# A decoder layer on one core: the way back's first four tiles normed together and turned chunk by chunk, the second gate's columns moved into the mixing

## The chip, the core and the metric

The kernel runs on one core of a Trainium2 chip. The core has a matrix engine (TensorE, PE in the profile; PEld is its weight load), VectorE (DVE), ScalarE (ACT), GpSimd (POOL) and SyncE (SP), whose queue issues most of the kernel's DMAs. The metric is the device time of one execution in microseconds, lower is better; several executions are timed and the median stands for the kernel.

## The reference

One hybrid decoder layer over 1024 tokens of width 1024, in float32. c is one conditioning vector; nine vectors of shifts, scales and gates come from it.

```python
mod = c_act @ w_ada + b_ada
(sh1, sc1, ga1, sh2, sc2, ga2, sh3, sc3, ga3) = jnp.split(mod, N_MOD, axis=-1)

h = modulate(rms_norm(x, g_pre_ff1), sh1, sc1)
f = swiglu(h, w1_gate, w1_up, w1_down)                 # 1024 -> 2816 -> 1024
x = x + 0.5 * ga1[:, None, :] * rms_norm(f, g_post_ff1)

h = modulate(rms_norm(x, g_pre_mix), sh2, sc2)
proj = h @ w_in                                        # q, k, v and u
attn = sliding_window_attention(q, k, v, sinks)        # window 128, 8 query heads, 2 kv heads
ssm = s5_ssm(u, ...)                                   # diagonal complex state space, GELU, GLU
mixed = jnp.concatenate([rms_norm(attn, g_attn_out), rms_norm(ssm, g_ssm_out)], -1) @ w_out
x = x + ga2[:, None, :] * rms_norm(mixed, g_post_mix)

h = modulate(rms_norm(x, g_pre_ff2), sh3, sc3)
x = x + 0.5 * ga3[:, None, :] * rms_norm(swiglu(h, w2_gate, w2_up, w2_down), g_post_ff2)
```

## The kernel before

The tokens are eight tiles of 128 (t = 0 to 7); the width is eight chunks of 128 (k = 0 to 7). Memory on the chip is divided by hand into named slots: `a0` to `a27`, `q`, `r`, `w` and `c0` hold 4 KB per partition, `h` and `t` 2 KB, and eight PSUM banks `b0` to `b7` hold 512 columns of float32 each. A tile asked for under a name waits until the last user of that slot is done. A planner works through the program with costs of its own and lays out one order of instructions for each engine ahead of time; on the chip every engine, and SP's queue of DMAs, keeps that order. `pinned` (line 85) ties instructions to the order in which they are written.

Each float32 product is made of three matmuls of rounded parts (`mm3`, lines 74 to 76). `split` (lines 69 and 70) makes the parts: ACT casts to the high part, DVE subtracts it from the source for the low part. So every operand that PE takes has first one pass of ACT and one of DVE.

The order of the work is: first half-step up (gate and up products), first way back (`down` with n = 0), mixing (`mix`), second half-step up, second way back (`down` with n = 2). Both half-steps use a scheme of seven products for a 2 by 2 block matrix product. The way back runs six of them ("1", "2", "6", "5", "3", "7"), each in 11 steps s of 12 matmuls, and the seventh in twelve pieces, three for each of tiles 4 to 7 (lines 621 to 639). The upper halves (`hi`, columns 512 to 1023) of tiles 0 to 3 are finished after "3" (line 612), so all of these four tiles stand in `f[0]` to `f[3]` before "7" begins. The upper halves of tiles 4 to 7 are finished after "7" (line 617), their lower halves piece by piece.

`epilogue` (lines 246 to 259) norms one whole tile: sum of squares on ACT, root and reciprocal in tiny steps (`rsqrt`, lines 141 to 145), product with the gate row `grow` on DVE, addition to x (line 255), store, and for n = 0 a second norm and a scaling (line 259) for the mixing. The four of them are listed in `todo` and run at odd steps of "7". `epilogue_half` (lines 261 to 288) does this for tiles 4 to 7, the upper half ahead of time with its gain product on POOL (line 269), the lower in `finish` after DVE copied PSUM into the tile (line 632).

For the mixing every tile is turned by PE (`to_mix`: four transposes into one bank, line 205), scaled and shifted into a staging tile, 128 columns at a time (ACT line 241, DVE line 243), and split into the operands `hm` (`split_mix`); tiles 0 to 3 share one staging tile and are split chunk by chunk when all four are in. `to_mix_` lists these steps, and the loop over the pieces takes one after each piece. The mixing then projects the first half of the tokens, which is tiles 0 to 3, with six weights (`project(i, 0)`), then the second half. The weights come through `ins`, a stream of loads (line 659) and splits; `before_mix` makes its first three loads and its first split, and is called after the tenth piece, with two small steps for the second gate before them.

`hook2` runs in each step of the way back. From the sixth step of "6" on it loads the second gate's weight columns (w_ada 40 to 47) as sixteen halves into `h` slots and reduces each with c on DVE (`ada_half`, line 171). The mixing's first loads into `a24` and `a25` are the attention's bias (line 736). Its scores begin after three projections of the second half.

Of the kernel before, what the change touches and what calls it, by code (L numbers as in the profile page):

```python
# [30 lines left out]
def tile_layer(ctx: ExitStack, tc: tile.TileContext, a: dict, out: bass.AP, stage: str = "all"):  # L31
# [212 lines left out]

    def split_mix(ts, stage, hm, ks):
        for k in ks:
            split(*(by_j(x[k], 16 * ts[0], 16 * len(ts)) for x in hm), by_j(stage[k], 0, 16 * len(ts)))
# [13 lines left out]
    def epilogue_half(n, t, f, grow, x_tag, j_tag, g_tag, normed):  # L261

        xt, junk, g = slot(x_tag, [D]), slot(j_tag, [D]), slot(g_tag, [D])
        sp.dma_start(xt, x_d[n][t])
        halves = slice(0, 512), slice(512, D)
        ss = small(2, "ssh")
        lo, hi = halves
        act.activation(junk[:, hi], f[:, hi], AF.Square, accum_out=ss[:, 1:2])
        pool.tensor_tensor(g[:, hi], f[:, hi], grow[:, hi], op=MUL)
        dve.tensor_scalar(ss[:, 1:2], ss[:, 1:2], 1.0 / D, EPS, op0=MUL, op1=ADD)  # L270

        def finish():
            act.activation(junk[:, lo], f[:, lo], AF.Square, accum_out=ss[:, 0:1])
            dve.tensor_tensor(g[:, lo], f[:, lo], grow[:, lo], op=MUL)
            v = small(1, "ssv")
            dve.scalar_tensor_tensor(v, ss[:, 0:1], 1.0 / D, ss[:, 1:2], op0=MUL, op1=ADD)
            r = rsqrt(v, 1)
            if normed:
                dve.scalar_tensor_tensor(xt, g, r[:, 0:1], xt, op0=MUL, op1=ADD)
                sp.dma_start(x_d[n + 1][t], xt)  # L280
                r = row_rstd(xt, f)
                act.activation(f, xt, AF.Identity, scale=r[:, 0:1])
            else:
                for h, eng in zip(halves, (sp, act)):
                    dve.scalar_tensor_tensor(xt[:, h], g[:, h], r[:, 0:1], xt[:, h], op0=MUL, op1=ADD)
                    eng.dma_start(x_d[n + 1][t][:, h], xt[:, h])

        return finish
# [211 lines left out]
    def down(n, wd, then, hook, last):  # L500
# [4 lines left out]
        raw_rots = [Rot(*names("a", 20, 21, 22, 23)), Rot(*names("a", 11, 12, 13, 14, 15, 27)), o_rot]  # L505
# [69 lines left out]
        todo = []  # L575
        for s in range(ns):
# [12 lines left out]
            if m == "7":  # L589
                late_ops[i] = slot(f"a{16 + i}", [2, 512], F32R)  # L590
                split(late_ops[i][:, 0], late_ops[i][:, 1], L[i][:, 1])
                if i % 2 and todo:
                    todo.pop(0)()
                if i == NH_F - 3:
                    upto("lload", 2, len(pieces), last_load)
                if i >= NH_F - 2:
                    upto("lconv", i - NH_F + 3, len(pieces), last_conv)
            if i < NH_F - 1:
                continue
            for t in range(4):  # L600
# [10 lines left out]
                elif m == "3":  # L611
                    dve.tensor_tensor(f[t][:, hi], f[t][:, hi], pbs[t], op=ADD)
                    if t == 0:
                        grow = load_row(n, "c0")
                    todo.append(lambda t=t: epilogue(n, t, f[t], grow, f"a{11 + t}", "a15", f"a{t}", then is not None))
                elif m == "7":
                    dve.tensor_tensor(f[4 + t][:, hi], f[4 + t][:, hi], pbs[t], op=ADD)
        for g in todo:
# [65 lines left out]
    def mix_streams():  # L684
# [8 lines left out]
        return Stream(ins, Rot(*names("r", 2, 3, 0, 1)), 3), Stream(us, Rot("w2", "w3"), 1), Stream(late, Rot("a14", "a15", "a14", "a15", "r0", "c0", "r0", "c0"), 1), Stream(shares, Rot(*names("w", 0, 1, 2, 3)), 3)  # L693

    def mix(hm, st, st_u, late, shares, todo, start):
# [25 lines left out]

        for j, i in enumerate(QKV):
# [721 lines left out]
    late_ada, late_raw = [(j, h) for j in range(40, 48) for h in range(2)], []  # L1444

    def hook2(s):

        i = s % NH_F
        if s < NH_F:
            if i == NH_F // 2:  # L1450
                for _ in prep[0]:
                    pass
# [11 lines left out]
    late_c = []  # L1464
# [7 lines left out]
    def to_mix_(f, t):  # L1472
# [4 lines left out]
        ts = [t for t in {0: (0, 1, 2, 3), 4: (4, 5), 5: (4, 5)}.get(t, (t,))]  # L1477
# [11 lines left out]
        todo = [lambda t=t, b=b: steps(t, b) for t in (ts if t == 0 else [t]) for b in range(2)]  # L1489
# [4 lines left out]
    def before_mix():  # L1494
        gate_row(1, 5, False)
        gate_store(1)
# [118 lines left out]
```

## Time and profile before

| | |
|---|---|
| median of 3 runs | 1712.78 us (1706.69 to 1713.24) |
| the profiled execution | 1704.67 us, span 1702.9 us |
| PE busy | 1649.9 us, 97% of the span |
| DVE, ACT, POOL busy | 1264.4 us (74%), 803.6 us (47%), 120.7 us (7%) |
| HBM | 145 GB/s over the span |

The span is the time from the first to the last instruction of the profiled execution. Busy times are sums over the whole layer, whose stages have different limits. In the rows below times are counted from the span's start.

### The profile page before, as it was taken

Reading aid. Unit: us, or ns where it says so; the run is one execution under the profiler, and the core shown is the slowest. Engines: PE = TensorE matmul, PEld = TensorE weight load, DVE = VectorE, ACT = ScalarE, POOL = GpSimd, SP = SyncE. Lnnn points to the kernel's source line nnn. Section 1 sums busy time; section 2 is a strip of 40 time slices with the busy share of each in tenths; the row PEclk is TensorE's granted clock in tenths of the full one; section 3 lists DMA queues with packets and bytes.
Section 4 is the critical chain, followed back from the end, with each engine's and each line's share of the span. In section 5 each row is a group of like instructions: output and inputs, shape, how many; then the busy total and the mean of one; then the engine's idle time right before and its main releaser. Section 6 shows DMA issues by size and latency. Waiting matters only on the chain.

```text
span 1702.9 us, 22218 instructions
## 1 busy us (share of the span) xinstructions
PE 1649.9 (97%) x7669; PEld 1353.3 (79%) x7669; DVE 1264.4 (74%) x2470; ACT 803.6 (47%) x1654; POOL 120.7 (7%) x147
## 2 busy tenths in 40 slices
PE   6999999999999999899989998999999999999998
PEld 5888888787788878788767886878888888888886
DVE  7999988789779878735589368777666566678586
ACT  5633333553344557736564257633333333444462
POOL 0011100001100000000014053000000000000001
PEclk8999999999999999999999998999999999999999
DMA  9186742234495733410233126253322223493324
GB/s 382 40 284 232 257 163 94 105 135 148 137 355 189 231 121 136 163 36 15 90 97 87 50 81 200 75 201 106 117 94 93 93 101 123 158 377 114 112 97 163
DMA packets 112066, 249.08 MB, mean 146 GB/s; under 512 B 12089, under 2 KB 27745, under 8 KB 111953
## 3 DMA queue, kind: packets, MB, share of 16 engines
q1 hardware_dynamic: 102224, 214.12, 36.6%
q0 software_dynamic: 9152, 32.49, 5.7%
q8 instruction: 60, 0.98, 0.2%
q10 hardware_dynamic: 576, 1.05, 0.2%
q14 instruction: 54, 0.43, 0.1%
HBM read 187.87 MB, written 59.75 MB: 145 GB/s over the span
## 4 chain that ended last, share of the span: by engine, by line
PE 50%; DVE 5%; ACT 2%; DMA 1%; issue 1%; SPq 0%; POOL 0%; DVEq 0%; ACTq 0%; POOLq 0%
PE b L76 15%; PE b L75 15%; PE b L74 15%; PE b L751 1%; PE b L839 1%; PE b L841 1%; DVE a L70 1%; PE b L840 1%; PE b L930 1%; PE b L785 1%; PE b L926 1%; ACT a L69 0%; PE b L205 0%; DMA r<-in_w_gu 0%; DMA w<-in_w_out 0%
## 5 line engine op out<-in xcount | busy, mean ns | idle before, releaser
L75 PE MATMUL b<-a,w 128*128 128x512 f32 x1260 | 493.5, 392 | 5.0 <-DVE a L70 5.0
L74 PE MATMUL b<-a,w 128*128 128x512 f32 x1260 | 489.2, 393 | 8.6 <-ACT w L69 3.5
L76 PE MATMUL b<-a,w 128*128 128x512 f32 x1260 | 494.2, 392 | 3.2 <-DVE w L70 3.1
L74 PEld LDWEIGHTS b<-a,w 128*128 128x128 f32 x1260 | 238.0, 189 | 61.6 <-ACT w L69 3.9
L76 PEld LDWEIGHTS b<-a,w 128*128 128x128 f32 x1260 | 238.3, 189 | 55.6 <-DVE w L70 5.9
L75 PEld LDWEIGHTS b<-a,w 128*128 128x128 f32 x1260 | 238.2, 189 | 55.1 <-DVE a L70 6.1
L70 DVE TENSOR_TENSOR w<-r,w 128x512 fp32r<-128x512 f32 (+1 forms) x206 | 142.9, 694 | 128.6 <-ACT w L69 128.3
L75 PE MATMUL b<-w,r 128*128 128x512 f32 x528 | 205.5, 389 | 1.7 <-DVE w L70 1.7
L76 PE MATMUL b<-w,r 128*128 128x512 f32 x528 | 205.4, 389 | 0.0
L74 PE MATMUL b<-w,r 128*128 128x512 f32 x528 | 180.7, 389 | 0.0
L69 ACT CAST w<-r 128x512 fp32r<-128x512 f32 (+1 forms) x210 | 130.2, 623 | 91.8 <-DVE r L334 82.1
L69 ACT CAST r<-a 128x512 fp32r<-128x512 f32 x110 | 68.5, 623 | 148.9 <-PE b L76 112.0
L70 DVE TENSOR_TENSOR r<-a,r 128x512 fp32r<-128x512 f32 x110 | 75.7, 688 | 60.3 <-ACT r L69 59.9
L75 PEld LDWEIGHTS b<-w,r 128*128 128x128 f32 x528 | 99.1, 188 | 22.7 <-DVE w L70 2.1
L76 PEld LDWEIGHTS b<-w,r 128*128 128x128 f32 x528 | 99.1, 188 | 20.6
L74 PEld LDWEIGHTS b<-w,r 128*128 128x128 f32 x528 | 99.1, 188 | 20.5
L69 ACT CAST w<-t 128x512 fp32r<-128x512 f32 (+1 forms) x114 | 69.9, 613 | 87.4 <-DVE t L337 33.5
L70 DVE TENSOR_TENSOR w<-t,w 128x512 fp32r<-128x512 f32 (+1 forms) x114 | 79.7, 699 | 32.4 <-ACT w L69 32.1
L466 DVE TENSOR_TENSOR h<-h,b 128x512 f32<-128x512 f32 x120 | 82.1, 685 | 20.4 <-PE b L76 18.6
L454 ACT ACTIVATE h<-h 128x512 f32<-128x512 f32 x60 | 38.0, 633 | 117.8 <-DVE h L466 117.8
L70 DVE TENSOR_TENSOR w<-a,w 128x512 fp32r<-128x512 f32 x110 | 75.4, 685 | 0.4 <-ACT w L69 0.4
L74 PE MATMUL b<-a,a 128*128 128x512 f32 x182 | 72.0, 398 | 0.0
(376 smaller groups left out, 2548.2 us busy)
## 6 DMA issues: line engine op xcount, KB each, us to landing
r<-in_w_gu SPq DMA_DIRECT2D x88, 512.0 KB, 4.1
g_d<-h SPq DMA_DIRECT2D x154, 256.0 KB, 2.2
a<-g_d SPq DMA_DIRECT2D x110, 256.0 KB, 3.4
q<-in_w_ada POOLq DMA_DIRECT2D x48, 512.0 KB, 4.6
a<-in_w_d SPq DMA_DIRECT2D x88, 256.0 KB, 5.4
a<-in_w_ada SPq DMA_DIRECT2D x16, 512.0 KB, 10.1
a<-in_x SPq DMA_DIRECT2D x12, 512.0 KB, 5.9
x_d<-a SPq DMA_DIRECT2D x12, 512.0 KB, 3.8
```

Source lines behind the costliest of these rows:

```text
L69: act.copy(hi, src)
L70: eng.tensor_tensor(lo, src, hi.bitcast(F32), op=SUB)
L74: pe.matmul(psum, wh, xh, start=first, stop=False, skip_group_check=goes_on)
L75: pe.matmul(psum, wh, xl, start=False, stop=False, skip_group_check=goes_on)
L76: pe.matmul(psum, wl, xh, start=False, stop=last, skip_group_check=goes_on)
L454: act.activation(dst, src, AF.Silu)
L466: dve.tensor_tensor(dst, dst, pb, op=ADD)
L751: pe.matmul(pb[kv][:, m % 2, ks], qT[m][rows, t * P : (t + 1) * P], kT[rows, (t + 1 - nk) * P : (t + 1) * P], start=True, stop=True,)
L785: pe.transpose(pt[:, m, :], pr[4 * kv + m][:, b * P : (b + 1) * P], ident)
L839: pe.matmul(pb, hh, wh, start=k == 0, stop=False)
L840: pe.matmul(pb, hh, wl, start=False, stop=False)
L841: pe.matmul(pb, hl, wh, start=False, stop=k == NK - 1)
```

## The change

Tiles 0 to 3 are no longer normed one by one. `epilogue_four` takes the sums of squares and gain products in halves: the lower halves while "5" runs, the upper in "7", each half in place in `f`; one root and reciprocal serves all four tiles, and a second one their second norm. Its steps are popped two at a step in "7". `to_mix_four` turns one chunk of all four tiles into one bank (`b4` to `b7`), evicts 512 columns by one instruction, on ACT or DVE in turn, and splits them at once; three such steps are popped after each of the first three pieces. `epilogue_half` works in place, makes its gain product on DVE and reads the lower half from PSUM without a copy. `before_mix` is called after the fifth piece.

The second gate's columns leave `hook2`. They are loaded whole, four at a time into `a24` to `a27`, in the mixing after the six projections of the first half, and reduced by `gate_columns` behind the remaining steps of the last tile, which are now pinned; the bias follows into `a24` and `a25`. The stream of projection weights has three slots instead of four. The slots of the "7" loads, of the half epilogues and of `grow` (loaded at the first step of "6") change with this. Both ways back use the new code; only the first has the second norm and the turning.

```diff
+    def to_mix_four(k, f, hm, rot):
+        pt = bank(f"b{4 + k % 4}", [4, P])
+        for t in range(4):
+            pe.transpose(pt[:, t, :], f[t][:, k * P : (k + 1) * P], ident)
+        stage = slot(rot(), [512])
+        dst = stage.rearrange("p (j t l) -> p t j l", j=8, t=4)
+        src = pt.rearrange("p t (j l) -> p t j l", j=8)
+        scale, shift = gsc[:, 1, k : k + 1], mod(3)[:, k : k + 1]
+        if k % 2:
+            dve.tensor_scalar(dst, src, scale, shift, op0=MUL, op1=ADD)
+        else:
+            act.activation(dst, src, AF.Identity, scale=scale, bias=shift)
+        split(*(by_j(x[k], 0, 64) for x in hm), by_j(stage, 0, 64))
...
+    def epilogue_four(n, f, grow, junks, x_tags, junk_tag, normed):
+        halves = slice(0, 512), slice(512, D)
+        ss = small(8, "ss4")
+        X = {}
+        def part(h, t):
+            junk = slot(junks(), [512])
+            act.activation(junk, f[t][:, halves[h]], AF.Square, accum_out=ss[:, 4 * h + t : 4 * h + t + 1])
+            dve.tensor_tensor(f[t][:, halves[h]], f[t][:, halves[h]], grow()[:, halves[h]], op=MUL)
+        def loads():
+            for t in range(4):
+                X[t] = slot(x_tags[t], [D])
+                sp.dma_start(X[t], x_d[n][t])
+        def first_norm():
+            v = small(4, "ssv4")
+            dve.tensor_tensor(v, ss[:, 0:4], ss[:, 4:8], op=ADD)
+            X["r"] = rstd_of(v, 4, D)
+            X["ss"] = small(4, "ssn4")
+        def add(t):
+            dve.scalar_tensor_tensor(X[t], f[t], X["r"][:, t : t + 1], X[t], op0=MUL, op1=ADD)
+            sp.dma_start(x_d[n + 1][t], X[t])
+            if normed:
+                act.activation(slot(junk_tag, [D]), X[t], AF.Square, accum_out=X["ss"][:, t : t + 1])
+        def second_norm():
+            X["r"] = rstd_of(X["ss"], 4, D)
+        def scaled(t):
+            act.activation(f[t], X[t], AF.Identity, scale=X["r"][:, t : t + 1])
...
         act.activation(junk[:, hi], f[:, hi], AF.Square, accum_out=ss[:, 1:2])
-        pool.tensor_tensor(g[:, hi], f[:, hi], grow[:, hi], op=MUL)
+        dve.tensor_tensor(f[:, hi], f[:, hi], grow[:, hi], op=MUL)
...
-        def finish():
-            act.activation(junk[:, lo], f[:, lo], AF.Square, accum_out=ss[:, 0:1])
-            dve.tensor_tensor(g[:, lo], f[:, lo], grow[:, lo], op=MUL)
+        def finish(pb):
+            act.activation(junk[:, lo], pb, AF.Square, accum_out=ss[:, 0:1])
+            dve.tensor_tensor(f[:, lo], pb, grow[:, lo], op=MUL)
...
-        raw_rots = [Rot(*names("a", 20, 21, 22, 23)), Rot(*names("a", 11, 12, 13, 14, 15, 27)), o_rot]
+        raw_rots = [Rot(*names("a", 20, 21, 22, 23)), Rot(*names("a", 11, 12, 13, 14, 15, 27)), Rot(*names("h", *range(6)))]
...
+        on_first, on_both = epilogue_four(
+            n, f, lambda: grow, Rot("h6", "h7"), names("a", 11, 12, 13, 14), "a15", then is not None)
...
-                if i % 2 and todo:
-                    todo.pop(0)()
+                for _ in range(2 if i < 6 else 1):
+                    if on_both:
+                        on_both.pop(0)()
...
+            if s == 2 * NH_F:
+                grow = load_row(n, "c0")
+            if m == "5" and i % 2 and on_first:
+                on_first.pop(0)()
...
-                tags = (f"q{t % 2}", "w3" if t < 2 else "q2", ("r0", "r2", "r3", "q3")[t])
+                tags = (("r0", "q0", "q1", "q0")[t], ("r3", "q2", "q3", "q2")[t])
...
-                dve.tensor_copy(y[:, lo], pb[0][t])
-                finish()
+                finish(pb[0][t])
...
-            if todo:
-                todo.pop(0)()
-            if s == len(pieces) - 3:
+            for _ in range(3 if s < 3 else 1):
+                if todo:
+                    todo.pop(0)()
+            if s == 4:
                 last()
...
-        return Stream(ins, Rot(*names("r", 2, 3, 0, 1)), 3), ...
+        return Stream(ins, Rot(*names("r", 2, 3, 0)), 2), ...
...
+        gate_ada, gate_raw = list(range(40, 48)), []
+        gate_rot = Rot(*names("a", 24, 25, 26, 27))
+        def gate_load(n_):
+            while gate_ada and len(gate_raw) < n_:
+                j = gate_ada.pop(0)
+                w = slot(gate_rot(), [D])
+                sp.dma_start(w, a["w_ada"][j])
+                gate_raw.append((j, w))
...
                 for f in todo[: 4 if j == 0 else None]:
-                    f()
+                    pinned(f)
                 todo = todo[4:]
+        gate_load(4)
         project(0, 1)
+        def gate_columns():
+            gate_c = load_c(sp)
+            for j in range(40, 48):
+                ada_block(*gate_raw.pop(0), gate_c)
+                gate_load(4)
+            gate_row(1, 5, False)
+        pinned(gate_columns, hold=False)
         project(1, 1)
+        gate_store(1)
...
-        elif s >= 2 * NH_F + 4:
-            if not late_c:
-                late_c.append(load_c(sp))
-            while late_ada and len(late_raw) < 4:
-                j, h = late_ada.pop(0)
-                w = slot(f"h{(2 * j + h) % 8}", [512])
-                tc.keep_in_program_order(sp.dma_start(w, a["w_ada"][j][:, 512 * h : 512 * h + 512]))
-                late_raw.append((j, h, w))
-            if s >= 2 * NH_F + 8 and late_raw:
-                ada_half(*late_raw.pop(0), late_c[0])
...
+            rot = Rot("h6", "h7")
+            return [lambda k=k: to_mix_four(k, f, hm, rot) for k in range(NK)]
...
     def before_mix():
-        gate_row(1, 5, False)
-        gate_store(1)
         ins.load(3)
         ins.conv(0)
```

## Rows read from the trace of the kernel before

**Rows 1.** The page, busy time of an engine, share of the span, instructions.

```profile
PE 1649.9 (97%) x7669; PEld 1353.3 (79%) x7669; DVE 1264.4 (74%) x2470; ACT 803.6 (47%) x1654; POOL 120.7 (7%) x147
```

**Rows 2.** Windows by stage: length, busy us (x count) by engine, granted clock, DMA.

```profile
595.50:625.50 30.00, 28.28 (x125) 23.08 (x124) 17.18 (x29) 14.42 (x27) 0.00 (x0) 1.00 0.53 167
625.50:655.50 30.00, 30.00 (x134) 24.83 (x133) 27.14 (x53) 22.31 (x41) 0.00 (x0) 1.00 0.10 40
655.50:690.85 35.35, 35.35 (x173) 29.45 (x172) 29.26 (x88) 27.84 (x68) 5.54 (x4) 1.00 0.56 181
690.85:705.25 14.40, 9.47 (x34) 7.35 (x33) 10.98 (x35) 11.46 (x24) 0.56 (x1) 0.76 0.79 268
...
729.90:754.00 24.10, 24.10 (x111) 19.44 (x111) 0.11 (x1) 3.00 (x6) 0.00 (x0) 1.00 0.13 44
```

**Rows 3.** Timeline of PE: start, length, line, operation, count, idle time before <-releaser.

```profile
690.85 0.27 PE L185 MATMUL b<-ident,ggc 128*8 128x128 f32 x1
690.96 0.60 PE L205 MATMUL b<-ident,q 128*128 128x128 f32 x4
695.03 0.50 PE L74 MATMUL b<-a,w 128*128 128x512 f32 x1 [3.47 <-ACT w L69]
...
697.66 0.80 PE L76 MATMUL b<-a,w 128*128 128x512 f32 x1 [1.46 <-DVE w L70]
...
703.22 0.39 PE L74 MATMUL b<-a,w 128*128 128x512 f32 x1
...
705.25 0.39 PE L74 MATMUL b<-a,q 128*128 128x512 f32 x1
```

**Rows 4.** Timeline of ACT, 689.0 to 698.5.

```profile
689.59 4.25 ACT L69 CAST a<-h 128x512 fp32r<-128x512 f32 x8
...
693.94 1.04 ACT L69 CAST w<-r 128x1024 fp32r<-128x1024 f32 x1
```

**Rows 5.** Timeline of DVE, 689.0 to 698.5.

```profile
696.40 1.21 DVE L70 TENSOR_TENSOR w<-r,w 128x1024 fp32r<-128x1024 f32 x1
```

**Rows 6.** Timeline of PE, 596.0 to 599.5.

```profile
598.89 0.50 PE L75 MATMUL b<-w,r 128*128 128x512 f32 x1 [1.72 <-DVE w L70]
```

**Rows 7.** Timeline of DVE, 593.0 to 600.0.

```profile
596.67 0.75 DVE L171 CUSTOM_DVE_ANT_0 h<-h,c,modc 128x512 f32<-128x512 f32 x1 [0.97 <-DMA h<-in_w_ada]
```

**Rows 8.** Timeline of all engines at the span's end.

```profile
1695.38 0.69 DVE L632 COPY q<-b 128x512 f32<-128x512 f32 x1 [1.76 <-PE b L76]
1696.11 0.63 ACT L273 ACTIVATE q<-q 128x512 f32<-128x512 f32 x1 [4.72 <-DVE q L632]
1696.11 0.69 DVE L274 TENSOR_TENSOR q<-q,c 128x512 f32<-128x512 f32 x1
...
1696.86 0.16 DVE L276 SCALAR_TENSOR_TENSOR s<-s 128x1 f32<-128x1 f32 x1
```

**Rows 9.** DVE's groups, 625.5 to 731: count | busy us, mean ns | idle before.

```profile
L243 DVE TENSOR_SCALAR h<-b,gsc,modc 128x128 f32<-128x128 f32 x28 | 9.7, 402 | 2.8 <-PE b L205 2.8
...
L255 DVE SCALAR_TENSOR_TENSOR a<-a,s,a 128x1024 f32<-128x1024 f32 x4 | 5.1, 1283 | 0.1
...
L254 DVE TENSOR_TENSOR a<-q,c 128x1024 f32<-128x1024 f32 x4 | 4.9, 1218 | 0.0
```

**Rows 10.** ACT's groups, the same stretch.

```profile
L241 ACT ACTIVATE h<-b,modc,gsc 128x128 f32<-128x128 f32 x28 | 10.5, 451 | 1.9 <-PE b L205 1.9
```

**Rows 11.** Line 166, whole gate columns: ns least/median/most, first and last start.

```profile
L166 DVE CUSTOM_DVE_ANT_0 q<-q,c,cols x48: 1276/1280/1286, 97.7 to 1169.3; 128x1024 f32<-128x1024 f32 x48
```

**Rows 12.** DMA issues, 680 to 760: count, KB each, median us to landing.

```profile
a<-in_k_bias SPq DMA_DIRECT2D x2, 512.0 KB, 5.9
```

**Rows 13.** DMA issues, 540 to 600.

```profile
h<-in_w_ada SPq DMA_DIRECT2D x16, 256.0 KB, 3.8
```

**Rows 14.** Timeline of ACT, 631 to 634.

```profile
631.48 1.28 ACT L141 ACT_TABLE_LOAD   x1
```

More of the change, by code (lines that the diff above doesn't have):

```diff
@@ L259, in epilogue, with epilogue_half @@
             act.activation(f, xt, AF.Identity, scale=r[:, 0:1])
-    def epilogue_half(n, t, f, grow, x_tag, j_tag, g_tag, normed):
-        xt, junk, g = slot(x_tag, [D]), slot(j_tag, [D]), slot(g_tag, [D])
+    def epilogue_four(n, f, grow, junks, x_tags, junk_tag, normed):
[24 more added lines that the diff above has]
+            act.activation(f[t], X[t], AF.Identity, scale=X["r"][:, t : t + 1])
+        on_first = [lambda t=t: part(0, t) for t in range(4)]
+        on_both = [loads] + [lambda t=t: part(1, t) for t in range(4)] + [first_norm] + [lambda t=t: add(t) for t in range(4)]
+        if normed:
+            on_both += [second_norm] + [lambda t=t: scaled(t) for t in range(4)]
+        return on_first, on_both
+    def epilogue_half(n, t, f, grow, x_tag, j_tag, normed):
+        xt, junk = slot(x_tag, [D]), slot(j_tag, [D])
         sp.dma_start(xt, x_d[n][t])
@@ L278, in finish @@
             if normed:
-                dve.scalar_tensor_tensor(xt, g, r[:, 0:1], xt, op0=MUL, op1=ADD)
+                dve.scalar_tensor_tensor(xt, f, r[:, 0:1], xt, op0=MUL, op1=ADD)
                 sp.dma_start(x_d[n + 1][t], xt)
@@ L284, in finish @@
                 for h, eng in zip(halves, (sp, act)):
-                    dve.scalar_tensor_tensor(xt[:, h], g[:, h], r[:, 0:1], xt[:, h], op0=MUL, op1=ADD)
+                    dve.scalar_tensor_tensor(xt[:, h], f[:, h], r[:, 0:1], xt[:, h], op0=MUL, op1=ADD)
                     eng.dma_start(x_d[n + 1][t][:, h], xt[:, h])
@@ L574, in down @@
         lo, hi = slice(0, 512), slice(512, D)
-        todo = []
+        on_first, on_both = epilogue_four(
+            n, f, lambda: grow, Rot("h6", "h7"), names("a", 11, 12, 13, 14), "a15", then is not None)
         for s in range(ns):
@@ L612, in down @@
                     dve.tensor_tensor(f[t][:, hi], f[t][:, hi], pbs[t], op=ADD)
-                    if t == 0:
-                        grow = load_row(n, "c0")
-                    todo.append(lambda t=t: epilogue(n, t, f[t], grow, f"a{11 + t}", "a15", f"a{t}", then is not None))
                 elif m == "7":
                     dve.tensor_tensor(f[4 + t][:, hi], f[4 + t][:, hi], pbs[t], op=ADD)
-        for g in todo:
+        for g in on_both:
             g()
@@ L692, in mix_streams @@
         shares = [(a["w_out"][4 + i], [D], *outs2[i], g_ssm[:, i : i + 1]) for i in range(4)]
-        return Stream(ins, Rot(*names("r", 2, 3, 0, 1)), 3), Stream(us, Rot("w2", "w3"), 1), Stream(late, Rot("a14", "a15", "a14", "a15", "r0", "c0", "r0", "c0"), 1), Stream(shares, Rot(*names("w", 0, 1, 2, 3)), 3)
+        return Stream(ins, Rot(*names("r", 2, 3, 0)), 2), Stream(us, Rot("w2", "w3"), 1), Stream(late, Rot("a14", "a15", "a14", "a15", "r0", "c0", "r0", "c0"), 1), Stream(shares, Rot(*names("w", 0, 1, 2, 3)), 3)
     def mix(hm, st, st_u, late, shares, todo, start):
@@ L1442, in hook1 @@
                 stored.append(0)
-    late_ada, late_raw = [(j, h) for j in range(40, 48) for h in range(2)], []
     def hook2(s):
[L1448 to L1452, printed above, removed]
-        elif s >= 2 * NH_F + 4:
-            if not late_c:
-                late_c.append(load_c(sp))
-            while late_ada and len(late_raw) < 4:
-                j, h = late_ada.pop(0)
-                w = slot(f"h{(2 * j + h) % 8}", [512])
-                tc.keep_in_program_order(sp.dma_start(w, a["w_ada"][j][:, 512 * h : 512 * h + 512]))
-                late_raw.append((j, h, w))
-            if s >= 2 * NH_F + 8 and late_raw:
-                ada_half(*late_raw.pop(0), late_c[0])
-    late_c = []
+        if s == NH_F // 2:
+            for _ in prep[0]:
+                pass
     g1.rest(hook1, pinned)
@@ L1476, in to_mix_ @@
                 hm[lo].extend(slot(f"a{8 * lo + k}", [D], F32R) for k in range(NK))
-        ts = [t for t in {0: (0, 1, 2, 3), 4: (4, 5), 5: (4, 5)}.get(t, (t,))]
+            rot = Rot("h6", "h7")
+            return [lambda k=k: to_mix_four(k, f, hm, rot) for k in range(NK)]
+        ts = {4: (4, 5), 5: (4, 5)}.get(t, (t,))
         stage = stages.setdefault(ts[0], [])
@@ L1487, in steps @@
             to_mix(t, f[t], stage, b, t - ts[0])
-        todo = [lambda t=t, b=b: steps(t, b) for t in (ts if t == 0 else [t]) for b in range(2)]
+        todo = [lambda b=b: steps(t, b) for b in range(2)]
         if t != 4:
```

## The prediction

> **What bounds the kernel now.** I read the page first. TensorE (PE) is busy 1649.9 of 1702.9 us [rows 1], so a change that leaves its matmuls alone, as this one does, can only return time in which PE stands still or runs at half clock. I then cut the span into the stretches that the change touches [rows 2]: the products "3" (595.5 to 625.5) and "7" (625.5 to 655.5) of the first way back, its end in twelve pieces (655.5 to 690.85), and the mixing's opening. In "7" and in the pieces PE has no idle time at all. "3" is busy 28.28 of 30.00, and the 14.40 us from 690.85 to 705.25 hold 9.47 us of PE at a granted clock of 0.76. The timeline of PE names that place [rows 3]: the way back's last matmul is followed at 690.85 by transposes, then PE waits 3.47 us for ACT and 1.46 us for DVE, and thirteen matmuls fill 697.66 to 703.22, 0.43 us each, where nine fill the 2.03 us from 703.22 to 705.25, 0.226 us each. That is the 1.2 GHz level against 2.4. What ends the waits last is seen on ACT and DVE [rows 4, 5]: eight casts that split tiles 0 to 3 for the projections run from 689.59, the cast of the first projection weight stands behind them at 693.94, and DVE subtracts that weight at 696.40. So tiles 0 to 3 are ready too late, although their products were finished at 625.5. The other idle time is one wait of 1.72 us at 598.89 for DVE [rows 6], and DVE was then held up by a reduction for the second gate whose 256 KB had not landed (0.97 us idle <-DMA, then 0.75 us) [rows 7]. At the end of the span the last tile's norm hangs bare behind the last matmul [rows 8].
>
> **The sum is made against the profiled execution**: 1704.67 us, a span of 1702.9 and 1.8 around it. It lies 8.1 us (0.5%) under the median of the three runs, 1712.78, so the change in us is carried over to that median. About 0.5%, 8.6 us, is what a measurement of this kernel can tell from no change.
>
> **Tiles 0 to 3 normed together and turned by chunk.** DVE's load decides whether it works. In "7" DVE is busy 27.14 of 30.00 [rows 2]. Out go four whole-row gain products, 4.9 us; in come four halves of 0.69 us each, priced at the half product's row (2.8) [rows 8], and at most all four additions of 5.1 us, some of which already stand there [rows 9]. That is 30.1 of 30.00 at most, before the six tiny runs of roots and reciprocals that the batch saves. So the additions end about at 655.5, and ACT's four scalings follow; DVE is full and PE is not touched as long as the splits for PE keep their place, which they did at 27.14. Then 32 evictions of 128x128 (16 at 451 ns on ACT, 16 at 402 ns on DVE [rows 9, 10]: 7.2 and 6.4 us) become eight of 128x512, at 0.63 and 0.69 us by the tail's rows [rows 8] 2.5 and 2.8 us. In the pieces DVE goes from 29.26 us by -3.6 (evictions), -2.7 (four copies dropped), +2.8 (half products taken over from POOL) and +5.5 (eight splits that stood in the stall) to 31.3 of 35.35, ACT from 27.84 by -4.7 and +5.3 to 28.4 [rows 2, 4]. Both fit, so tiles 0 to 3 and the first weight, whose load and split are moved from the tenth piece to the fifth, should be ready ten us or more before 690.85. PE's transposes stay 32.
>
> What the first projection then returns: 705.25 - 690.85 = 14.40 us, less its 24 matmuls at 0.226 (5.4) and nine transposes between them (about 1.0): **8.0 us**. Below: nothing, if another wait takes the place; above: 9.0, if the transposes leave too. I take 8.0 because PE's other stretches with the same mix of matmuls and transposes, the pieces, have no idle time.
>
> **Second gate's columns.** Sixteen loads of 256 KB and sixteen half reductions of 0.75 us leave the way back; four first halves of the batch (0.69 each) come into product "5". The wait at 598.89 goes with them: **1.7 us**, bounds 0 and 1.72. In the mixing they come back as eight loads of 512 KB on SP's queue, one of c, a Silu on ACT, eight reductions of 1.28 us [rows 11], one small product, a transpose, a copy and a store on POOL. DVE is busy 0.11 us and ACT 3.00 us of the 24.10 us from 729.90 to 754.00 [rows 2], which hides 10.5 us of DVE work; the transfers move 4 MB in a stretch that runs at 44 GB/s. Cost 0, as long as the attention's bias, which now waits for the same two slots, is there when DVE takes up the first scores (now 754.0, then about 744): behind tile 7's last steps the reductions can begin at 721 at the latest (before that the second half can't be projected either), four of them take 5.2, the next loads 5.9 by the slower landing [rows 12, 13], two more reductions 2.6, the bias 5.9: 741. It is close, hence a rival below. Without that cover the price is us for us.
>
> A table load on ACT took 1.28 us when Sqrt followed the gates' functions [rows 14]; Silu among the square roots of tiles 4 to 7 brings one or two more, hidden by the same 21 us of idle ACT.
>
> **Half epilogues from PSUM.** After the last matmul DVE's copy of 0.69 us goes: the square on ACT and the product on DVE start at 1695.38 instead of 1696.11, which gives 0.73 us if they run beside each other as they now do [rows 8]. If the two readers of one bank are put one behind the other, the square's 0.63 comes before the product's 0.69, the sum of squares is taken up after 1.4 us instead of 1.48 (1696.86 - 1695.38), and 0.1 is left. I take the middle, **0.4 us**. The Trainium skill, "PSUM — Partial Sum Buffer", section "PSUM bank collisions raise a hardware error", says that two engines must not touch one bank at the same time, reads included, and that software orders them; by that rule the gain is the 0.1, and no row of before shows two engines reading one bank at once.
>
> **New waits of PE**: between 0 (the pieces as they are) and 4.9 (both waits of 690.96 again); nearest is the row of the pieces, so I add 0.5 us.
>
> Sum: -8.0 - 1.7 - 0.4 + 0.5 = **-9.6 us**: 1695.1 for an execution like the profiled one, **1703.2** on the scale of the median; own range -11.4 (9.0 + 1.7 + 0.7) to -5.2 (waits of 4.9), so 1701.4 to 1707.6.
>
> **Rivals.** *The stall moves instead of going.* DVE at 30 of 30 in "7" lets the batch run over; all four tiles must now be scaled before the first chunk can be turned, and transposes placed too early in PE's order, or splits late on DVE, stop PE inside the pieces. For it: the order is laid out by a planner ahead of time, and DVE's 27.14; against: no idle PE in 655.5 to 690.85. A new wait like 690.96's, with its half clock, returns 4 to 7 us of the 9.6: about 1709, anywhere from 1706 to 1711. That the change doesn't do what it says (the lo halves still late) ends here too, at 1712.
>
> *The gate's columns hold up the attention* (the other side). If the loads land one after another behind SP's waits, the bias comes at 721 + 8 x 3.8 + 2 x 5.9 = 763 instead of 744 [rows 12, 13], and the attention, with PE behind it, is 19 us late: -9.6 + 19 = +9.4, or 1722. It decides from a bias that lands 10 us late. Against it: loads of one round overlap, and the stretch has bandwidth to spare.
>
> *More comes back than that*: with the attention planned anew, part of PE's idle time in the mixing goes too; -12 to -16, 1699.
>
> **Chances.** Forecast 0.62, moved stall 0.21, attention held up 0.10, more 0.07. The forecast's middle lies just beyond the 8.6 us, so of its 0.62 I count 0.43 as faster by over 0.5% and 0.19 within; with the last rival faster is 0.50. Within 0.5%: 0.19 + 0.21 = 0.40. Slower: 0.10. The range takes in the forecast, the moved stall up to 1711, and the three runs' own spread (6.5 us, mostly below their median): 1696 to 1712.
>
> **What would show it.** Right: PE goes on at 690.85 with projections at 0.226 us and full clock; no ACT or DVE wait there; "3" without its 1.72 us; DVE's reductions for the gate inside its idle time before the first scores; the tail shorter by one DVE copy. Wrong: PE idle inside the pieces, released by ACT or DVE for the chunks; a first-scores wait for the bias; DVE-bound stretches in the second way back's "5" and "7", whose epilogues changed too and which have no idle PE to give.

## The result and the profile after

| | before | after |
|---|---|---|
| median of 5 runs each, beside each other | 1709.45 us (1706.69 to 1713.24) | 1692.25 us (1691.59 to 1698.31) |
| ratio, 95% interval | | 0.9906 [0.9884, 0.9928] |
| profiled execution, its mean granted clock | 1704.67 us, 0.988 | 1698.31 us, 0.987 |

The change makes the kernel faster by 17.2 us (1709.45 - 1692.25); the interval, times 1709.45, reaches from 12.3 to 19.8. Run once more, it gave 1692.87 us and 0.9890 [0.9874, 0.9905]. The forecast was 9.6 less, at 1703.2, with 1696 as the range's lower end: the direction was right, the size wrong. Note the table's last line: the two profiled executions lie only 6.4 us apart, because before's was faster than each of its five timed runs and after's was the slowest of its five. That turns out to be the centre of the case.

The page of after, busy time, and its windows by stage (busy us by engine, then the granted clock, the DMA share and GB/s):

```profile
PE 1650.6 (97%) x7669; PEld 1354.7 (80%) x7669; DVE 1254.8 (74%) x2407; ACT 802.4 (47%) x1650; POOL 107.8 (6%) x139
```

```profile
595.00:625.00 30.00, 30.00 (x134) 24.86 (x133) 16.22 (x25) 16.47 (x31) 0.00 (x0) 1.00 0.39 120
625.00:655.00 30.00, 30.00 (x134) 24.83 (x133) 27.80 (x51) 24.40 (x48) 0.00 (x0) 1.00 0.33 118
655.00:690.00 35.00, 35.00 (x175) 29.20 (x174) 26.94 (x66) 24.81 (x52) 0.00 (x0) 1.00 0.55 171
690.00:705.00 15.00, 15.00 (x76) 12.58 (x75) 13.50 (x35) 13.71 (x31) 0.00 (x0) 1.00 0.98 368
...
720.00:744.50 24.50, 24.50 (x114) 19.97 (x114) 9.29 (x18) 3.24 (x8) 0.53 (x1) 1.00 0.50 172
```

Set beside [rows 2], PE has no idle time left from 595 to 705: product "3" is full where it was 28.28 of 30.00, and the stretch behind the way back, 9.47 us of PE in 14.40 at a clock of 0.76 before, is 15.00 of 15.00 at full clock. DVE is no fuller in "7" than 27.80 of 30.00. The busy sum of PE is the same to 0.7 us: nothing was taken off it.

PE's timeline of after, where the way back's last matmul (operand r, the last piece) meets the first projection (operand w), and the projections' 25th matmul:

```profile
691.15 0.39 PE L76 MATMUL b<-a,r 128*128 128x512 f32 x1
691.37 0.39 PE L74 MATMUL b<-a,w 128*128 128x512 f32 x1
...
693.19 1.03 PE L205 MATMUL b<-ident,q 128*128 128x128 f32 x8
...
697.71 0.39 PE L74 MATMUL b<-a,w 128*128 128x512 f32 x1
```

The projection starts 0.22 us behind the way back, the pace of any two matmuls, where it waited 3.47 and 1.46 us [rows 3]. The first 24 projection matmuls with the transposes between them take 6.3 us (697.71 - 691.37), where 14.40 us went by. Why they can is seen on ACT:

```profile
654.47 4.27 ACT L309 ACTIVATE q<-a,s 128x1024 f32<-128x1024 f32 x4
661.19 0.78 ACT L257 ACTIVATE h<-b,modc,gsc 128x512 f32<-128x512 f32 x1 [0.92 <-PE b L249]
```

and on DVE:

```profile
654.59 1.22 DVE L70 TENSOR_TENSOR w<-r,w 128x1024 fp32r<-128x1024 f32 x1 [1.40 <-ACT w L69]
661.30 0.81 DVE L255 TENSOR_SCALAR h<-b,gsc,modc 128x512 f32<-128x512 f32 x1 [0.18 <-PE b L249]
...
675.25 0.68 DVE L70 TENSOR_TENSOR a<-h,a 128x512 fp32r<-128x512 f32 x1
```

The four scalings end at 658.74, the first projection weight is split at 655.8, and the last chunk of tiles 0 to 3 at 675.9: 15 us ahead of the projection. Before, the weight's split began at 696.40 [rows 5], 5.5 us behind the way back's end. The eviction of 512 columns costs 0.78 and 0.81 us; I had taken 0.63 and 0.69 from the tail.

DVE's timeline in the mixing, the second gate's columns and the first scores (line 841):

```profile
719.06 1.28 DVE L166 CUSTOM_DVE_ANT_0 a<-a,c,cols 128x1024 f32<-128x1024 f32 x1 [0.82 <-ACT c L118]
...
728.40 1.29 DVE L166 CUSTOM_DVE_ANT_0 a<-a,c,cols 128x1024 f32<-128x1024 f32 x1 [0.91 <-DMA a<-in_w_ada]
...
731.03 0.17 DVE L181 TENSOR_TENSOR ggc<-modc,cols 128x8 f32<-128x8 f32 x1
744.47 0.69 DVE L70 TENSOR_TENSOR a<-b,a 128x512 fp32r<-128x512 f32 x1 [13.28 <-ACT a L69]
745.08 0.34 DVE L841 CUSTOM_DVE_ANT_0 a<-b,a,sink 128x128 f32<-128x128 f32 x1
```

All eight reductions fit between 719 and 731, DVE waits twice for a column to land, under a microsecond each time, and it is then idle for 13 us. The scores begin at 745.08 (I expected about 744), with no wait for the bias. The rival in which the columns hold up the attention did not come.

### The profile page after: what moved, and what is told of

It reads as the page before. It is cut to its first block, busy times and chain, and to the rows that moved or that the text cites. A ratio compares the mean times of both kernels' runs of the same rounds, so it can differ in the third digit from the quotient of the medians.

```text
span 1696.4 us, 22121 instructions
## 1 busy us (share of the span) xinstructions
PE 1650.6 (97%) x7669; PEld 1354.7 (80%) x7669; DVE 1254.8 (74%) x2407; ACT 802.4 (47%) x1650; POOL 107.8 (6%) x139
## 4 chain that ended last, share of the span: by engine, by line
PE 86%; DVE 7%; ACT 3%; issue 1%; DMA 1%; POOL 0%; SPq 0%; DVEq 0%; ACTq 0%; POOLq 0%
PE b L76 26%; PE b L75 26%; PE b L74 26%; PE b L831 1%; PE b L919 1%; PE b L921 1%; PE b L1010 1%; PE b L920 1%; PE b L865 1%; DVE a L70 1%; DVE w L70 1%; DVE h L485 1%; PE b L1006 1%; DMA r<-in_w_gu 1%; PE b L207 1%
```

## The experiments

Each ratio is against before, run on the same chip in turn. "Half-clock stretch" is a stretch in which the trace shows PE granted 1.2 GHz in place of 2.4. The first group asks which part of the change carries the gain. My theory: tiles 0 to 3, scaled as the pieces begin. Rivals: the pace of three steps after a piece, the weight's earlier split, or the turning by chunk.

**Gates alone.** before, with only the second gate's columns moved:

```diff
+        gate_load(4)
         project(0, 1)
...
+        pinned(gate_columns, hold=False)
         project(1, 1)
+        gate_store(1)
...
-        elif s >= 2 * NH_F + 4:
-            if not late_c:
...
-                ada_half(*late_raw.pop(0), late_c[0])
```

> The kernel before with the second gate's columns alone moved into the mixing (pinned behind tile 7's steps, as in the change). Theory 1: the wait of 1.72 us at 598.9 goes, the one at 691 stays: -1.7 us and at most -3, ratio 0.998 to 0.999. Rival (the 4 MB of gate loads or their sixteen reductions cost the way back more than the trace shows): -5 us or more, ratio 0.997 or below. If the gate's columns held up the attention, as the losing rival of the forecast had it: +5 or more.

1713.70 us, ratio 0.9993 [0.9975, 1.0012]. The wait at 599 is gone, the one behind the way back is not (PE's timeline of this run):

```profile
689.82 0.93 PE L205 MATMUL b<-ident,q 128*128 128x128 f32 x7
695.02 0.80 PE L74 MATMUL b<-a,w 128*128 128x512 f32 x1 [4.28 <-ACT w L69]
```

So the median doesn't show what the trace gives back. The executions fall into two groups: 1704 to 1708 us at a mean granted clock of 0.986 to 0.987, and 1713 to 1715 at 0.980 to 0.982. The profiled one, of the second kind, has half-clock stretches of 10.2 us from 693.7 and 30.7 us from 881.5.

**Pace alone.** before, with three of the old steps after each of the first three pieces:

```diff
-            if todo:
-                todo.pop(0)()
+            for _ in range(3 if s < 3 else 1):
+                if todo:
+                    todo.pop(0)()
```

> The kernel before with one line changed: three steps of the mixing's turning are taken after each of the first three pieces instead of one. Theory 2 (the list's pace alone put the splits of tiles 0 to 3, its ninth and tenth step, behind the ninth and tenth piece, and that was the stall): the wait at 691 goes, with its half clock, and the ratio comes to 0.993 to 0.995; the wait at 599 stays. Theory 1 (the tile by tile norm is what is late, tile 3 scaled at 678): PE waits still, at 691 or inside the pieces, and the ratio stays above 0.997.

1707.61 us, 0.9987 [0.9974, 1.0001]; PE still stops three times:

```profile
699.37 0.80 PE L74 MATMUL b<-a,q 128*128 128x512 f32 x1 [2.36 <-ACT q L69]
...
702.95 0.80 PE L76 MATMUL b<-a,w 128*128 128x512 f32 x1 [1.06 <-DVE w L70]
...
713.01 0.50 PE L74 MATMUL b<-a,q 128*128 128x512 f32 x1 [2.03 <-ACT q L69]
```

Asking earlier for steps whose tiles aren't normed yet moves the wait a little. The pace isn't the cause.

**Pace taken back.** after, with one step after a piece (the same lines the other way round).

> The change with one step per piece instead of three in the first three. Theory 2: the eight chunks are turned and split after pieces one to eight, in time for the first projection, but tiles 4 to 7 move back behind them; a wait of PE at 690 of 0 to 2 us, ratio 0.990 to 0.993. Theory 1 (norm in time is enough): no wait, ratio 0.9895 as for the change. If pace is all that counts: the wait of 5 us is back, ratio 0.995 or more.

1703.23 us, 0.9940 [0.9917, 0.9963]: the median is 11 us above after's, with no wait behind the way back. The place of the loss is below, with the clock.

**Weights late.** after, with the weights' first loads and split where they were:

```diff
-            if s == 4:
+            if s == len(pieces) - 3:
                 last()
```

> The change, but with the first projection weights loaded and split after the tenth piece, as before, instead of the fifth. Theory 1 (both the tiles' split and the weight's cast were late, and each alone would hold PE): PE waits 1 to 3 us for the weight's split after the last piece, and runs at half clock for some us behind it: +2 to +6 us against the changed kernel, ratio to before 0.992 to 0.995. Rival (only the tiles were late): no wait, ratio 0.9906 as for the change.

1694.73 us, 0.9893 [0.9873, 0.9913], no wait. The earlier place is not needed.

**Turned tile by tile.** after, with the old `to_mix` steps for tiles 0 to 3:

```diff
-            rot = Rot("h6", "h7")
-            return [lambda k=k: to_mix_four(k, f, hm, rot) for k in range(NK)]
-        ts = {4: (4, 5), 5: (4, 5)}.get(t, (t,))
+        ts = [t for t in {0: (0, 1, 2, 3), 4: (4, 5), 5: (4, 5)}.get(t, (t,))]
```

> The change, but tiles 0 to 3 turned as before: 32 evictions of 128x128 tile by tile and eight splits behind all of them; normed together as in the change. Theory 1 (the batch norm alone frees enough): splits end before 690, no wait of PE, ratio 0.990 to 0.992. Rival (the turning by chunk matters): evictions take 7.2 and 6.4 us instead of 2.5 and 2.8, the splits end after 690 and PE waits 1 to 4 us again: ratio 0.993 to 0.996.

1693.91 us, 0.9888 [0.9868, 0.9908], no wait. The turning by chunk is not needed either.

**Normed one by one.** after, with the old whole-tile epilogues for tiles 0 to 3:

```diff
-        on_first, on_both = epilogue_four(
-            n, f, lambda: grow, Rot("h6", "h7"), names("a", 11, 12, 13, 14), "a15", then is not None)
+        on_both = []
...
-                for _ in range(2 if i < 6 else 1):
-                    if on_both:
-                        on_both.pop(0)()
+                if i % 2 and on_both:
+                    on_both.pop(0)()
```

> The change with tiles 0 to 3 normed one by one as before (whole rows, one step at every odd step of product 7), turning by chunk, three per piece. Theory 1: tile 3 is scaled near 678 again, no chunk can be turned before, so PE waits inside the pieces or at 690 by 2 to 5 us, with half clock: ratio 0.993 to 0.997. Theory 2: the turning steps pull the norms forward, no wait of PE: ratio 0.989 to 0.991.

1707.09 us, 0.9976 [0.9965, 0.9987]: most of the gain is gone. PE's timeline of this run:

```profile
710.41 0.63 PE L205 MATMUL b<-ident,q 128*128 128x128 f32 x4 [1.48 <-DVE h L243]
711.61 0.66 PE L205 MATMUL b<-ident,q 128*128 128x128 f32 x4 [0.57 <-ACT h L241]
...
719.04 0.48 PE L828 MATMUL b<-a,a 64*128 64x128 f32 x2 [1.34 <-ACT a L770]
720.08 1.24 PE L205 MATMUL b<-ident,q 128*128 128x128 f32 x7 [0.55 <-ACT q L338]
```

The fourth tile's scaling ends at 675.2 in this run, against 678.9 in before and 658.7 in after. The stall at 691 does not return in its place; the late work is pushed on to the turning of tiles 4 to 7, and 5.22 us of waiting stand at 884.14. So the batch carries most of the gain, because its tiles are scaled 16 us earlier, as the pieces begin. This edit takes away its early start in "5" and its pace together with it; which of these matters most was not tested. My theory stands, in a weaker form than I had: the turning, the pace and the weight's place could each be put back by itself without a wait behind the way back. All of them put back at once, the batch alone, was not tried.

**Old half epilogues.** after, with the copy from PSUM, the gain product on POOL and the old slots:

```diff
-        dve.tensor_tensor(f[:, hi], f[:, hi], grow[:, hi], op=MUL)
+        pool.tensor_tensor(g[:, hi], f[:, hi], grow[:, hi], op=MUL)
...
-                finish(pb[0][t])
+                dve.tensor_copy(y[:, lo], pb[0][t])
+                finish()
```

> The change with the half epilogues of tiles 4 to 7 as before in both ways back: gain product of the upper half on POOL, DVE's copy of the lower half, the old slots. Theory 1 (the batch norm of tiles 0 to 3 removes the wait by itself): no wait at 690, the tail longer by 0.2 us, ratio as for the change to within 0.001. Rival (the freed DVE copies and the product taken from POOL are part of it): PE waits 1 us or more between 655 and 725, ratio 0.992 or more.

1696.47 us, 0.9906 [0.9890, 0.9921]. The pieces are not longer (33.7 us from their first matmul to the first projection, as in after); two waits of 0.31 and 0.38 us come at 703 to 705, and the first 154 matmuls from the first projection on take 1.9 us more (39.97 against 38.09). The median lies 3.6 us above that of after on the same chip (1692.87, below): more than the theory allowed, less than the rival. The mean granted clock was high besides (0.990); the product of time and clock, used further down, is 1679.2 us, 4.4 above after's, and no execution of the one reaches the other's range. So the new half epilogues carry part of the gain too. Where, beyond those 1.9 us and 0.2 at the span's end, was not followed up.

**Copy alone put back.** after, with DVE's copy ahead of `finish`, which works on the tile in place:

```diff
-                finish(pb[0][t])
+                dve.tensor_copy(y[:, lo], pb[0][t])
+                finish(y[:, lo])
```

> The change with DVE's copy out of PSUM put back ahead of the lower half's square and product. From the traces, the two readers of one bank already run one behind the other, so from the last matmul to the sum of squares the tail goes from 1.37 us back to 1.5: +0.15 us, not to be seen in the time (ratio as for the change to within 0.001). Had the two run beside each other, it would be +0.7.

1695.27 us, 0.9898 [0.9883, 0.9914]. The tail grows by 1.0 us, not by the 0.15 expected. The rows of DVE, then of ACT, in the timeline of this run's end:

```profile
1683.47 0.69 DVE L691 COPY q<-b 128x512 f32<-128x512 f32 x1 [2.77 <-PE b L76]
1684.95 0.69 DVE L330 TENSOR_TENSOR q<-q,c 128x512 f32<-128x512 f32 x1 [0.79 <-ACT q L329]
...
1684.20 0.63 ACT L329 ACTIVATE q<-q 128x512 f32<-128x512 f32 x1 [5.72 <-DVE q L691]
```

In place, the product overwrites what the square reads, so it waits for the square (0.79 us) and the copy's 0.69 comes on top. I had overlooked that.

The second group asks where the gain beyond the forecast comes from.

**Before again**, unchanged, for its spread; and four more profiles of it.

> The kernel before, unchanged, as a control. Theory 1 (waits and half-clock stretches): its executions scatter by some 6 to 9 us (1704 to 1713) with the profiled 1704.67 at the low end, and the longer ones show the lower mean granted clock, about 0.001 for every 1.7 us, because the half-clock stretch after the wait at 691 is of different length from execution to execution. Rival (something else than the clock makes the unprofiled executions longer): the mean clock stays at 0.988 while the times scatter.

1709.98 us (1705.45 to 1715.83 in 12 runs), 0.9986 [0.9969, 1.0002]. The time follows the mean granted clock: 1705.45 us at 0.987, 1715.83 at 0.982.

> The kernel before, one more profile. If the change's extra gain comes from the wait at 691: in executions with a mean clock of 0.984 or less the half-clock stretch behind 691 is 15 us or longer. If it comes from the attention's end: that of 691 stays at 6.8 us and the one near 880 is 20 to 30 us.

> As the look before it: the half-clock stretch that grows with a falling mean clock is either the one behind 691 (the change removes it) or the one near 880 (both kernels have it).

> As the first look: stretch behind 691 against stretch near 880, in an execution whose mean clock decides how much it tells (0.984 or less tells it apart).

> As the first look: stretch behind 691 against stretch near 880, in an execution whose mean clock decides how much it tells (0.984 or less tells it apart).

1719.5, 1708.62, 1708.27 and 1710.84 us, at mean clocks of 0.979, 0.985, 0.983 and 0.984. Here is one stretch, the attention's end, in the windows of the profile of before that I predicted from:

```profile
868.00:880.00 12.00, 8.73 (x80) 6.99 (x79) 12.00 (x30) 9.61 (x32) 0.55 (x1) 1.00 0.39 131
880.00:908.00 28.00, 24.59 (x161) 18.54 (x161) 28.00 (x42) 18.64 (x39) 11.21 (x12) 0.88 0.39 114
```

and in the first of the four profiles, with the stretch behind the way back:

```profile
695.00:710.00 15.00, 9.57 (x32) 7.24 (x31) 11.66 (x35) 12.23 (x28) 0.56 (x1) 0.66 0.78 269
...
880.00:908.00 28.00, 22.73 (x79) 16.95 (x75) 24.98 (x40) 14.43 (x36) 5.95 (x5) 0.60 0.27 85
```

The two windows from 880 don't hold the same work: the second execution is 5 us behind by then. Counted by instruction, the 160 that PE starts between 882.36 and 908.01 in the first, 25.7 us, take 34.4 us in the second (886.38 to 920.77). In the trace's record of the clock the half-clock stretch near 880 lasts 6.8 us in the profile that I read, and 13.7, 27.3, 13.7, 17.1 and 17.1 us in the five others. The one near 697 lasts 6.8, 6.8, 10.2, 6.8, 6.8 and 6.8. So it is the one near 880 that lengthens as the mean clock falls, not the one behind 691 as I had expected of the control. I had read the mildest of six.

**After again**, unchanged.

> The changed kernel once more, on the chip of the next three, for its clock. Theory 1: us times mean clock stays at 1675 to 1676 in every execution (before: 1684 to 1686), the mean clock lies near 0.989 and the scatter follows it; ratio 0.988 to 0.992. Rival (the first five executions were a lucky set): the mean clock comes down to before's 0.985 and the ratio up to 0.994.

1692.87 us (1692.33 to 1694.73), 0.9890 [0.9874, 0.9905]; no half-clock stretch near 697, 10.2 us near 868. In after's first profile, windows:

```profile
700.00:866.00 166.00, 164.88 (x876) 132.44 (x874) 96.50 (x317) 95.47 (x311) 1.52 (x7) 1.00 0.24 80
866.00:888.00 22.00, 17.32 (x56) 12.38 (x56) 20.19 (x34) 12.93 (x34) 5.95 (x5) 0.61 0.29 96
```

and in that of the kernel with one step after a piece:

```profile
700.00:866.00 166.00, 164.88 (x870) 131.94 (x869) 97.97 (x319) 94.88 (x310) 1.53 (x7) 1.00 0.24 77
866.00:902.00 36.00, 31.02 (x107) 23.17 (x107) 25.49 (x41) 17.51 (x43) 9.05 (x10) 0.57 0.31 90
```

PE's busy time from 700 to 866 is the same to the hundredth; then one stays at half clock for 17.1 us and the other for 30.7. Five of the latter's eight runs show a mean clock of 0.982 to 0.983, and those at 0.990 to 0.991 take 1696 us. In both the stretch begins behind PE's waits near 867 and 869; why it lasts so long here I can't say.

**Filling the attention's wait.** after, with the state product placed one block later, into those waits:

```diff
         n = more(n)
-        ss_state(1)
         n = more(n)
+        ss_state(1)
         ss_out(0)
```

> The change with one exchange in the mixing: the second state step of the state space part is taken behind the attention's turning of its last tile instead of ahead of it. It aims at the waits near 866 to 875, after which the half-clock stretch lasted 6.8 to 30.7 us in the profiles so far. Theory 3 (this stretch makes most of the scatter between executions): with fewer waits there the half-clock stretch is short, mean clock 0.990 or more in all executions, spread under 4 us and ratio 0.986 to 0.988. Rival: the waits move on to the state space part, ratio 0.989 to 0.991 and the same scatter.

1695.95 us (1694.60 to 1702.65), 0.9916 [0.9897, 0.9935]. The half-clock stretch near 867 shrinks to 3.4 us, other waits come, and the spread of the clock (0.985 to 0.991) is not smaller. No gain.

**The output weights' splits held.** after, with these splits pinned behind the attention's last step:

```diff
-            if n < NT + 3:
+            if n == NT + 2:
+                pinned(at, n)
+            elif n < NT + 2:
                 at(n)
...
-                wo.extend(late.get(i) for i in range(4))
+                wo.extend(pinned(late.get, i, hold=False) for i in range(4))
```

> The change with the splits of the output weights held behind the attention's last step (pinned). In the trace of the change four of them, 1.27 us each on DVE, stand among the last attention steps near 864 to 889, where PE waits. Theory 3 (waits there set off the long half-clock stretch): PE's waits of 866 to 875 shrink by 1 to 2 us, the half-clock stretch is under 10 us, mean clock 0.990 or more, ratio 0.986 to 0.988. Rival: the weights are late for the products behind them, PE waits there instead; ratio 0.990 or more.

1701.72 us, 0.9942 [0.9925, 0.9958]. PE's timeline:

```profile
868.41 0.50 PE L74 MATMUL b<-h,a 128*128 128x512 f32 x1 [3.06 <-DVE a L993]
869.39 0.49 PE L74 MATMUL b<-h,a 128*128 128x512 f32 x1 [0.47 <-ACT h L69]
872.08 0.80 PE L75 MATMUL b<-h,a 128*128 128x512 f32 x1 [2.20 <-DVE h L70]
```

The waits stay and a new one of 3.01 us comes at 927.18, when the held splits are needed. The waits at the attention's end are not due to these splits standing ahead.

## Why the prediction was off

To see where the time went I set the same matmuls of six profiles of before beside those of five profiles of the changed kernel and of its variants without a new wait (after twice, weights late, turned tile by tile, copy put back), and took the means:

```
stretch                          before    after   difference
with the wait at 599              84.1     81.6      -2.5
way back's end                    51.7     50.9      -0.8
start of the mixing               49.1     41.2      -7.9
on to the attention              134.7    134.0      -0.7
attention's end                   62.9     61.1      -1.8   (60.2 to 67.8; 59.6 to 63.2)
second half-step, its start       56.5     55.3      -1.2
span                            1708.4   1693.6     -14.8
```

**The stall behind the way back** was forecast at 8.0 and measured 8.7 (7.9 and 0.8 of the pieces); on the forecast's own terms, in the profiles that I read, it is 8.1 (14.40 against 6.34). Its mechanism was right: tiles ready too late, and with them ready 15 us early no wait. Of the means by which I got there, the batched norm is the one that can't be put back.

**The second gate's columns** were forecast at 1.7 and 2.5 came; their cost in the mixing was nothing, as forecast, with DVE done at 731 against the 741 that I had reckoned. Moved by themselves they gave back the wait, though the median didn't fall (0.9993).

**The tail** was forecast at 0.4 between 0.1 and 0.73. After's timeline of the end:

```profile
1689.07 0.60 ACT L329 ACTIVATE q<-b 128x512 f32<-128x512 f32 x1 [5.63 <-PE b L76]
1689.56 0.19 ACT L329 ACTIVATION_READ_ACCUMULATOR q<-b 128x1 f32 x1
1689.79 0.69 DVE L330 TENSOR_TENSOR q<-b,c 128x512 f32<-128x512 f32 x1 [4.13 <-ACT q L329]
1690.40 0.15 DVE L332 SCALAR_TENSOR_TENSOR s<-s 128x1 f32<-128x1 f32 x1
```

DVE's product starts when ACT has read the same bank, accumulator included, so the sum of squares is taken up 1.33 us after the square's start (1690.40 - 1689.07), against 1.48 [rows 8]: 0.15. The rule of the Trainium skill, "PSUM — Partial Sum Buffer", section "PSUM bank collisions raise a hardware error", that two engines don't touch one bank together and are put in order by software, agrees with these rows. The lower bound of 0.1 was the right one, not the middle that I took. But the tail is not all that the half epilogues are worth: put back as they were, they cost 4.4 us by the product of time and clock.

**New waits** were given 0.5; in the pieces and behind them there are none.

These terms make 11.4 (2.5 + 8.7 + 0.2) against 9.6, and two differences of the table that I had not costed add 1.9 (0.7 and 1.2). So for an execution like the profiled one I forecast 1695.1, and the mildest of after took 1691.59: 3.5 us less, about the 3.7 that these make (1.8 + 1.9). That alone would have given 1699.7 on the median's scale, inside the range.

**The step that failed is the one that I put first: the sum is made against the profiled execution, which "lies 8.1 us (0.5%) under the median of the three runs, 1712.78, so the change in us is carried over to that median".** It treats the 8.1 us as a constant that the changed kernel would have too. It has 0.7: its median, 1692.25, stands that far above its mildest run. The two pieces, 3.5 and 7.4 (8.1 - 0.7), make the 10.9 us between 1703.2 and 1692.25. The median of three was not at fault: 60 runs of before in the comparisons had a median of 1711.86.

What the 8.1 us are is shown by the granted clock. The time of an execution multiplied by its mean granted clock counts a microsecond at half clock as half. This product hardly moves: 1685.0 us on average over those 60 runs (1681.9 to 1688.7, where the times go from 1705.88 to 1717.94), 1684.2 for the profiled execution, 1679.2 to 1683.5 for the four single profiles, and 1674.9 over after's ten. It is 1675.5 for weights late and for turned tile by tile, 1676.6 even for the slow kernel with one step after a piece, 1679.2 for the old half epilogues, 1681.2 for the gates alone, 1683.3 for the pace alone, 1684.6 with the tiles normed one by one. So 10 us of the gain are work and waits that are gone whatever the clock, and by this measure the gates alone did give back 3.8, which a lower clock (0.9824 on average) took away.

The mean clock of the 60 runs was 0.9843, of after's ten 0.9889. At 0.9843 after would take 1674.9 / 0.9843 = 1701.6, 10.3 less than before's mean of 1711.9; the other 7.9 us, down to its mean of 1693.7, go with the clock. Up to 4 of them belong to the half-clock stretch near 697, a mean of 7.4 us in six profiles at half the work, which goes with the wait and was in my 8.0. The other 4 or more lie elsewhere. The table's traces place 1.8 of them at the attention's end, where PE's waits are the same in both (4.5 us on average before, 4.7 after), so that the clock alone makes the difference. Where the rest lies is not shown. The attention's end is also where the profile that I read had its shortest half-clock stretch: 6.8 us against a mean of 16 over the six, up to 4.6 us of time ((16 - 6.8) / 2), and 2.7 by the table (62.9 - 60.2).

**What stays open:** whether that stretch is shorter in after by something the change did (17.1 and 10.2 us in its two profiles), and so why its median stands so close to its mildest run. Two kernels that differ in their pace alone, one of them 1.3 us behind the other by 866 and without a new wait until then, differ by 11 us in their medians, so an effect of something small is possible; filling the waits and holding the splits did not bring it out. The 1.2 us at the second half-step's start also came with the gates alone; there one wait of 0.8 us is missing, and I didn't follow why.

Of the rivals, "more comes back than that" gave 1699 and named "part of PE's idle time in the mixing"; it is the nearest, with too small a figure, and its reason holds only if the attention's end is counted to the mixing. The moved stall and the late bias did not come. DVE and ACT in the pieces were forecast at 31.3 and 28.4 us of 35.35 and were busy 26.94 and 24.81 of 35.00; the evictions I priced too low, the whole too high, and neither bore on the end.

## What to carry to other kernels

A profile is one execution: before a sum is carried to a median, set the granted clock of the profiled execution beside that of the timed ones, and price each place where PE waits and falls to half clock from several executions. To compare kernels whose clocks scatter, set time multiplied by mean granted clock beside the medians; here its mean stayed within 1684.8 to 1686.0 for before in sets of 11 to 25 runs, and ranked variants whose medians the clock had mixed. And when a batch replaces a string of small steps, ask which of the parts makes its consumer's data early: here the norm did, and the turning, the pace and the weight's place could each be put back without a new wait (the pace not without a slower median, 1703.23).

## What the runs showed that I had not expected

- The same program, with the same waits of a few microseconds at the attention's end, was granted 1.2 GHz there for 6.8 us in one execution and 27.3 us in another; over the whole span the mean clock was 0.988 and 0.979, and the time 1704.67 and 1719.5 us. In the first the clock was back 5.0 us after the last wait there, in the second 22.9 us after it, with PE busy all that while.
- Evicting four turned blocks, 128x512, with scale and shift and in a permuted order took 0.78 us on ACT and 0.81 on DVE, against 0.60 and 0.69 for 128x512 read straight from PSUM in the tail. Which of the two costs the difference no run separates.
- The two engines that read one bank in the tail ran one behind the other: DVE started 0.72 us after ACT (1689.79 - 1689.07), behind a square of 0.60 and the read of its accumulator, 0.19.
